# A hand-written planner for one Trainium2 core: new figures for durations, latencies and transfers, four projection tiles taken out of pairs, and another engine choice for late weight splits

## The chip, the cores and the metric

The kernel runs on one core of one Trainium2 chip. Time is device microseconds (us) of that core; lower is better. The engines are TensorE (PE, with its weight loads shown as PEld), VectorE (DVE), ScalarE (ACT), GpSimd (POOL) and SyncE (SP), which issues nearly all DMAs.

## The reference

One pre-norm layer over 512 tokens of 1024 channels with two token mixers in parallel, fed by one input projection. Cut to what matters:

```python
h = rmsnorm(x, norm_g)
(q_lat, c_kv, k_rope, z_a, q_b, k_b, v_b, z_b,
 q_idx, k_idx, w_idx, gate_a, gate_b) = split(h @ w_in)
# A: latent attention, 8 heads of 64 (+32 rotary), dense, chunk-causal
y_a = mla_attention(...) * silu(z_a)
# B: indexer scores, top 128 keys a query, T5 bias, 8 heads of 64
y_b = dsa_attention(...) * silu(z_b)
merged = sigmoid(gate_a) * (y_a @ w_o_a) + sigmoid(gate_b) * (y_b @ w_o_b)
out = rmsnorm(x + merged @ w_out, final_g)
```

All is float32. `z_b`, the gate path of the second mixer, is 512 channels wide: four tiles of 128 channels, called ZB here.

## The kernel before, in words

**Arithmetic.** A float32 operand is held as two parts: `hi`, the value rounded to PE's one-pass float32 format by an ACT cast (L370), and `lo = x - hi` by a subtraction on DVE (L401) or GpSimd (L403). A product is three matmuls, hi*hi, hi*lo and lo*hi (`mm3`). All weights come from HBM in float32 into four buffers `raw`, are split into slots `s_w` or `s_wo`, multiplied, and the slots freed. Slots are 73 tiles of 128 x 512 that every class of data shares (`SB`); PSUM has 8 banks, with limits by use.

**Stages.** Early projections (latents, indexer) from x; the normalised input `hT`; then a list of jobs (`QUEUE`): gate tiles `ga`/`gb`, gate paths `za`/`zb`, first-mixer weights `ma`, `va`, `pe`, second-mixer q and k `sb`, values `VB`; in between, the heads of both mixers; then `w_o` (16 jobs), and `w_out` as seven products (Strassen-Winograd, `out_job`, products 1 to 7), residual, final norm, output.

**Plain tiles and pairs.** A name in small letters in `QUEUE` is a plain tile (`proj`): 8 steps of k, three matmuls of 512 columns each. Two names in capitals form a pair (`proj2`): two tiles by 512 tokens are done as a 2 x 2 block product with seven half-size products, of 4 k steps and three matmuls of 256 columns each (`seven`). A pair needs sums of weight blocks (DVE or GpSimd), seven splits, sums of input blocks (`input_sums`, made once for all pairs, tiles `s_hs`), evictions of partial results (ACT) and two additions from PSUM (DVE). `silu2` finishes a ZB tile: tanh on ACT, one multiply on DVE; from PSUM for a plain tile, from SBUF for a pair.

**What sets the order.** No scheduler of the compiler does. The program's generator threads run through a planner (`Flow.run`) when the kernel is built: each step has an engine or a choice of engines and an assumed duration; the planner keeps when each engine comes free, adds a latency from engine to engine (`lat`) and a model of the DMA queue, and emits the step that it thinks can start first, weighted by a thread's priority. The order of emission is the order on each engine's in-order queue. For a step with a choice (`BOTH`: DVE or GpSimd) it takes the engine that ends first; `pbias` is added to GpSimd's end (0 by `soon`; `flow.pbias` where none is given, which becomes `LATE` after the last top-k). Two-input DVE steps and GpSimd steps exclude each other in the model (`shares`, `port`). In the model's figures `dur` of a DMA is its bytes at 360 GB/s.

**Names used further on.** `lg` banks hold attention logits (L1894 to L1896, exp by ACT L379); L498 are transposes; L413 is a scalar-tensor-tensor step on DVE; `s_wsum` sums of weight blocks; `bias_scratch<-s_sig` spills a gate tile to HBM, because `AWAY` holds all eight; `SUMS_AT` names the head after which `input_sums` starts, `PSUMS` its priority; `YSB` a head that releases the first mixer's output splits; `PHCAP`, `PCAP`, `SPARE` limit slots; `OUT_AT` says after which `w_o` jobs a `w_out` job is put; `PTOPK`, `PSCORE` are priorities (smaller is first).

Of the kernel before, what the change touches and what calls it, by code (L numbers as in the profile page):

```python
# [15 lines left out]
AF = mybir.ActivationFunctionType  # L16
# [137 lines left out]
class Flow:  # L154
    @staticmethod
    def lat(src, dst):

        if src == dst or src == "SP" or src is None:
            return 0.0
        if dst == "PE":  # L160
            return 0.26
        return {"PE": 0.2, "ACT": 0.15, "DVE": 0.16, "POOL": 0.08}[src]

    def __init__(self, order):
        self.free = {"PE": 0.6, "ACT": 0.73, "DVE": 0.93, "POOL": 0.73, "SP": 0.73}
# [48 lines left out]
    def run(self, stop=None):  # L214
        while self.threads:
# [36 lines left out]
            if eng == "SP":  # L252

                self.free["SP"] = s + 0.05
                self.hw = max(self.hw, s) + (0.65 if step.ins and step.outs else 0.475)
                self.dma = max(self.dma, self.hw + 0.65) + dur * (SLOWER[bool(step.ins and step.outs)] if s > 25.0 else 1.0)
                end = self.dma + (LAND if step.ins and step.outs else 1.5 if s < 0.77 or dur < 0.05 else 2.15 if s < 10.0 else 1.8 if s < 20.0 else 1.0) + step.late
            else:
                self.free[eng] = end = s + dur
                if self.shares(step, eng):  # L260
                    self.port, self.holder = end, eng
                    if eng == "DVE":
                        self.paired, self.pair = end, step.made
# [21 lines left out]
YIELD = 0.15  # L285
SWITCH = 0.1
JITTER = 0
SEED = 687
DRAWN = random.Random(SEED)
TC_ARGS = {}  # L290

# [2 lines left out]
def tile_block(ctx: ExitStack, tc: tile.TileContext, a: dict, out: bass.AP, bias_dram: bass.AP):  # L294
# [67 lines left out]
    def bufs(*vs):  # L362
        return [v.buf for v in vs if isinstance(v, View)]

    def act_opt(dst, src, func=AF.Copy, scale=None, bias=None, accum=None):
        t = (0.05 if in_ps(src) else 0.1) + 0.00083 * src.n + ((0.18 if in_ps(src) else 0.09) if accum is not None else 0) + (0.09 if isinstance(scale, View) else 0)

        def emit():
            if func == AF.Copy and scale is None:
                nc.scalar.copy(dst.ap, src.ap)  # L370
            else:
                kw = {}
                if scale is not None:
                    kw["scale"] = sc(scale)
                if bias is not None:
                    kw["bias"] = sc(bias)
                if accum is not None:
                    kw["accum_out"] = sc(accum)
                nc.scalar.activation(dst.ap, src.ap, func, **kw)  # L379

        return ("ACT", t, emit)
# [11 lines left out]
    def soon(step):  # L393
        step.pbias = 0.0
        return step

    def tt(dst, x, y, op, engs=("DVE",)):
        opts = []
        for e in engs:
            if e == "DVE":  # L400
                opts.append(("DVE", 0.07 + 0.00104 * x.n, lambda: nc.vector.tensor_tensor(dst.ap, x.ap, y.ap, op=op)))  # L401
            else:
                opts.append(("POOL", 0.15 + 0.0021 * x.n, lambda: nc.gpsimd.tensor_tensor(dst.ap, x.ap, y.ap, op=op)))  # L403
# [12 lines left out]
        return step  # L416

    def ts(dst, x, s1, s2, op0, op1=None):
        t = 0.1 + (0.00104 if in_ps(x) else 0.00052) * x.n
        kw = {} if op1 is None else {"op1": op1}  # L420
        step = Step([("DVE", t, lambda: nc.vector.tensor_scalar(dst.ap, x.ap, sc(s1), s2, op0, **kw))],
                    bufs(dst), bufs(x, s1))
        step.pair = not in_ps(x) and x.n > 8
        return step

    def scale_by(dst, x, s, engs=BOTH):

        opts = []
        for e in engs:
            if e == "DVE":  # L430
                t = 0.1 + (0.00104 if in_ps(x) else 0.00052) * x.n
                opts.append((e, t, lambda: nc.vector.tensor_scalar(dst.ap, x.ap, s.ap, None, ALU.mult)))
            elif e == "POOL":
                opts.append((e, 0.25 + 0.00083 * x.n,
                             lambda: nc.gpsimd.tensor_scalar(dst.ap, x.ap, s.ap, 1.0, ALU.mult, ALU.mult)))
            else:
                opts.append(act_opt(dst, x, AF.Copy, s))
        step = Step(opts, bufs(dst), bufs(x, s))
        step.pair = not in_ps(x)
        return step  # L440
# [27 lines left out]
        return step  # L468

    def stream(n):  # L470
        return max(0.0148 + n / 2400, 0.109) - 0.0015 * (n == 256)

    def mm(ps, pairs, start, stop, more=False):

# [17 lines left out]
    def turn(parts):  # L492


        def emit():
            for d, s in parts:
                product_to(d, True)
                nc.tensor.transpose(d.ap, s.ap, ident.tile)  # L498

        return pe(0.109 * len(parts), [d for d, _ in parts], [s for _, s in parts] + [ident.all], emit, len(parts))  # L500

    def dma(dst, src):

# [460 lines left out]
    def topk(i):  # L964

        n = P * (i + 1)
        work = mask_in_order(i)
        for r in range(TOPK // 8):
            m8 = yield Get(SMALL)
            t = 0.07 + 0.00104 * n  # L970
            yield Step([("DVE", t, lambda: nc.vector.max(m8.tile, work.ap))], [m8], [mask[i]])  # L971
            yield Step([("DVE", t + 0.068, lambda: nc.vector.match_replace(work.ap, m8.tile, work.ap, MARK))], [mask[i]], [m8])  # L972
            put(m8)
        yield ts(work, work, MARK, MASK, ALU.not_equal, ALU.mult)
        done.add(("mask", i))
# [1149 lines left out]
    def split_b(raw, key, last):  # L2125
        hi = yield slot("wo", 32)
        lo = yield slot("wo", 32)
        yield act(hi.all, raw)
        yield soon(lo_part(lo.all, raw, hi.all))
        if last:  # L2130
            put(raw.buf)
        right[key] = (hi, lo)
# [1 line left out]
    def out_job(product, c):  # L2134
# [3 lines left out]
        def prep(job):  # L2138
# [11 lines left out]
            else:  # L2150
                for i in range(2):
                    yield Until(lambda: 2 * c + i in sums)
                    t = sums[2 * c + i].all.f
                    yield soon(tt(t, raw[i], t, ALU.add if product == 6 else ALU.subtract, BOTH))
                    if i == 1:
                        put(job.raw)
                    yield from split_b(t, (product, 2 * c + i), product == 4)
# [405 lines left out]
```

## Time and profile before

| | us |
|---|---|
| median of 3 runs | 425.13 |
| lowest, highest | 423.97, 425.34 |
| the profiled execution | 425.56 |
| its span, first to last instruction | 423.8 |
| PE, DVE, ACT, POOL busy in it | 413.6, 378.7, 297.5, 100.9 |

The granted TensorE clock is 0.996 over the span. The page of the profile gives busy time by engine, the chain of work that ended last, groups of instructions and DMA issues; the trace behind it answers by stretch of time, by engine and by tile. A group's row reads: line, engine, operation, output<-inputs with buffer numbers left out, shapes, count, then busy us, mean ns of one, idle us of the engine before them and what ended that idle time. A row of the timeline reads: start us, length us, engine, line, operation, count, and in brackets the idle time before. A row of waits: who waited, for whom, total us, times, longest. A row of a stretch: its length, busy us of PE, PEld, DVE, ACT and POOL with instruction counts, granted clock, DMA share, GB/s. A matmul's end is modelled, and a matmul overlaps its neighbours in PE's pipeline, so the distance from start to start is what one costs.

### The profile page before, as it was taken

How to read it: one execution, taken by the hardware profiler on the slowest of the kernel's cores; microseconds unless marked ns; L12 is line 12 of the kernel's file. 1: busy time of each engine (PE TensorE's matmuls, PEld its weight loads, DVE VectorE, ACT ScalarE, POOL GpSimd, SP SyncE). 2: the span in 40 equal slices, each digit the busy share in tenths (PEclk: the TensorE clock that was granted, in tenths of full speed). 3: DMA queues.
4: the chain of work that ended last, by engine and by line, in shares of the span. 5: the costliest groups of instructions: out<-in, count | busy, mean ns of one | idle time of the engine just before them, and what ended most of it. 6: DMA issues, size and time to landing. Idle time of an engine off the chain costs nothing.

```text
span 423.8 us, 7541 instructions
## 1 busy us (share of the span) xinstructions
PE 413.6 (98%) x2487; PEld 368.8 (87%) x2487; DVE 378.7 (89%) x804; ACT 297.5 (70%) x682; POOL 100.9 (24%) x127
## 2 busy tenths in 40 slices
PE   9999999999999999999999999999999999999983
PEld 6999888898887888889999999999998888888863
DVE  4879789899999999997999789899869997999994
ACT  5796976479584967749786798997689744347534
POOL 1033764024344547541000012130001000010212
PEclk9999999999999999999999999999999999999998
DMA  8973345724644631442334737314633975566305
GB/s 266 394 285 101 116 137 183 182 57 110 202 104 152 179 111 49 125 113 76 113 130 105 200 95 199 95 65 136 187 113 125 336 254 200 182 201 209 134 1 199
DMA packets 30279, 65.91 MB, mean 156 GB/s; under 512 B 4648, under 2 KB 5688, under 8 KB 30240
## 3 DMA queue, kind: packets, MB, share of 16 engines
q1 hardware_dynamic: 29120, 63.82, 48.1%
q0 software_dynamic: 832, 1.22, 1.1%
q8 instruction: 19, 0.31, 0.3%
q10 hardware_dynamic: 288, 0.39, 0.3%
q14 instruction: 20, 0.16, 0.1%
HBM read 50.49 MB, written 4.21 MB: 129 GB/s over the span
## 4 chain that ended last, share of the span: by engine, by line
PE 65%; DVE 20%; ACT 5%; issue 4%; DMA 2%; POOL 1%; SPq 1%; POOLq 0%; DVEq 0%; ACTq 0%
PE ps L479 57%; PE ps L498 4%; DVE s_wo L401 2%; DVE s_mg L401 2%; ACT s_w L370 2%; DVE s_w L401 1%; DVE s_wsum L401 1%; DMA raw<-w_out 1%; DVE s_rg L401 1%; DVE s_x L413 1%; DVE mask L972 1%; DVE s_pair L401 1%; PE ps L606 1%; PE ps L946 1%; DVE s_xr L413 1%
## 5 line engine op out<-in xcount | busy, mean ns | idle before, releaser
L479 PE MATMUL ps<-s_h,s_w 128*128 128x512 f32 (+1 forms) x672 | 139.2, 350 | 0.0
L479 PEld LDWEIGHTS ps<-s_h,s_w 128*128 128x128 f32 x672 | 106.6, 189 | 13.4 <-ACT s_w L370 0.2
L370 ACT CAST s_w<-raw 128x512 fp32r<-128x512 f32 (+3 forms) x134 | 77.4, 596 | 18.5 <-DVE raw L401 9.3
L401 DVE TENSOR_TENSOR s_w<-raw,s_w 128x512 fp32r<-128x512 f32 (+2 forms) x104 | 67.1, 663 | 6.9 <-ACT s_w L370 6.2
L479 PE MATMUL ps<-s_hs,s_w 128*128 128x256 f32 x384 | 53.5, 285 | 0.0
L403 POOL TENSOR_TENSOR s_w<-raw,s_w 128x512 fp32r<-128x512 f32 (+2 forms) x30 | 35.0, 1173 | 77.6 <-DVE s_ys L413 36.9
L479 PEld LDWEIGHTS ps<-s_hs,s_w 128*128 128x128 f32 x384 | 49.2, 191 | 0.4
L479 PE MATMUL ps<-s_ys,s_w 128*128 128x512 f32 x192 | 43.7, 389 | 0.0
L479 PEld LDWEIGHTS ps<-s_ys,s_w 128*128 128x128 f32 x192 | 36.0, 188 | 7.6
L479 PE MATMUL ps<-s_wo,s_mg 128*128 128x512 f32 (+1 forms) x156 | 33.6, 374 | 1.2 <-ACT s_wo L370 0.9
L479 PEld LDWEIGHTS ps<-s_wo,s_mg 128*128 128x128 f32 x156 | 27.6, 188 | 7.0 <-ACT s_wo L370 1.3
L479 PE MATMUL ps<-s_w,s_xg 128*128 128x328 f32 (+1 forms) x192 | 32.9, 324 | 0.1
L479 PEld LDWEIGHTS ps<-s_w,s_xg 128*128 128x128 f32 x192 | 31.3, 188 | 0.6 <-ACT s_rbc L370 0.5
L379 ACT ACTIVATE s_p<-s_p,sm 128x512 f32<-128x512 f32 (+3 forms) x58 | 31.6, 564 | 0.1
L972 DVE MATCH_REPLACE8 mask<-sm,mask 128x256 f32<-128x256 f32 (+2 forms) x48 | 25.8, 540 | 0.0
L971 DVE MAX8 sm<-mask 128x8 f32<-128x256 f32 (+2 forms) x48 | 25.5, 547 | 0.3
L498 PE MATMUL ps<-ident,s_p 128*128 128x128 f32 x160 | 23.0, 274 | 0.0
L379 ACT ACTIVATE s_p<-ps,sm 128x128 f32<-128x128 f32 (+3 forms) x32 | 16.7, 525 | 8.9 <-DVE sm L1878 8.8
L370 ACT COPY s_tmp<-ps 64x512 f32<-64x512 f32 (+1 forms) x18 | 10.1, 562 | 15.5 <-PE ps L479 8.7
L498 PEld LDWEIGHTS ps<-ident,s_p 128*128 128x128 f32 x160 | 18.4, 140 | 2.6 <-DVE s_ph L401 0.5
L479 PE MATMUL ps<-s_lat,s_w 128*128 128x512 f32 x78 | 20.5, 394 | 0.0
L1977 DVE CUSTOM_DVE_ANT_0 s_p<-ps,mask 128x128 f32<-128x128 f32 (+3 forms) x32 | 15.3, 486 | 4.9 <-PE ps L479 4.7
(217 smaller groups left out, 798.4 us busy)
## 6 DMA issues: line engine op xcount, KB each, us to landing
raw<-w_out SPq DMA_DIRECT2D x18, 512.0 KB, 5.2
s_op<-s_op SPq DMA_DIRECT2D x36, 128.0 KB, 2.4
raw<-w_ga SPq DMA_DIRECT2D x8, 512.0 KB, 3.4
raw<-w_gb SPq DMA_DIRECT2D x8, 512.0 KB
raw<-w_o SPq DMA_DIRECT2D x16, 256.0 KB, 4.5
s_x<-xT SPq DMA_DIRECT2D x8, 256.0 KB, 4.0
s_xn<-x SPq DMA_DIRECT2D x8, 256.0 KB, 5.6
raw<-w_za SPq DMA_DIRECT2D x4, 512.0 KB, 5.0
```

Of the source, the lines that this page charges most:

```text
L370: nc.scalar.copy(dst.ap, src.ap)
L379: nc.scalar.activation(dst.ap, src.ap, func, **kw)
L401: opts.append(("DVE", 0.07 + 0.00104 * x.n, lambda: nc.vector.tensor_tensor(dst.ap, x.ap, y.ap, op=op)))
L403: opts.append(("POOL", 0.15 + 0.0021 * x.n, lambda: nc.gpsimd.tensor_tensor(dst.ap, x.ap, y.ap, op=op)))
L413: lambda: nc.vector.scalar_tensor_tensor(dst.ap, x.ap, sc(s), y.ap, op0=op0, op1=op1))],
L479: nc.tensor.matmul(ps.ap, l.ap, r.ap, start=start and i == 0, stop=stop and i == len(pairs) - 1, skip_group_check=more)
L498: nc.tensor.transpose(d.ap, s.ap, ident.tile)
L606: nc.tensor.matmul(ps.tile.rearrange("p (a b) -> p a b", b=P), z, z.rearrange("p (a b) -> p a b", a=1).to_broadcast([P, NT, P]), start=Tru ...
L946: yield pe(0.005 + n / 2400, [ps.all], [qs[h].all, ks[0].all], lambda: (product_to(ps[:, :n], True), nc.tensor.matmul(ps.tile[:, :n], qs[h ...
L971: yield Step([("DVE", t, lambda: nc.vector.max(m8.tile, work.ap))], [m8], [mask[i]])
L972: yield Step([("DVE", t + 0.068, lambda: nc.vector.match_replace(work.ap, m8.tile, work.ap, MARK))], [mask[i]], [m8])
L1977: step = Step([("DVE", 0.1 + 0.00104 * n, lambda: nc.vector.tensor_tensor_reduce(p.ap, ps.tile[:, :n], mask[i].tile, op0=ALU.add, op1=ALU. ...
```

## The change

It has three parts. The planner's figures: engine latencies, durations of some kinds of step, the DMA model after 25 us. The four ZB tiles: `ZB0` to `ZB3` (two pairs) become `zb0` to `zb3` (plain), at other places of the list. The engine choice of `w_out`'s sums and low parts: `soon` becomes `late`, which gives products 1, 7, 2, 6 and 5 a bias of 0 as before, and 4 and 3 the bias `LATE`; `LATE` itself goes from 0.75 to 0.4. Beside these, settings of priorities, slot limits and positions move.

```diff
 lat:
-            return 0.26
-        return {"PE": 0.2, "ACT": 0.15, "DVE": 0.16, "POOL": 0.08}[src]
+            return TO_PE
+        return {"PE": 0.2, "ACT": 0.14, "DVE": 0.12 if dst == "ACT" else 0.16, "POOL": 0.08}[src]
 run, a step of SP:
-                self.hw = max(self.hw, s) + (0.65 if step.ins and step.outs else 0.475)
-                self.dma = max(self.dma, self.hw + 0.65) + dur * (SLOWER[bool(step.ins and step.outs)] if s > 25.0 else 1.0)
-                end = self.dma + (LAND if step.ins and step.outs else 1.5 if s < 0.77 or dur < 0.05 else 2.15 if s < 10.0 else 1.8 if s < 20.0 else 1.0) + step.late
+                kind = 0 if step.ins and step.outs else 1 if step.outs else 2
+                if s > 25.0:
+                    at = max(self.hw, s)
+                    self.hw = at + 0.59
+                    self.dma = max(self.dma, at + 1.0) + dur * SLOWER[kind]
+                    end = self.dma + LAND[kind] + step.late
...
+    def few(x):
+        return 0.12 if x.ap.shape[0] < P else 0
 act_opt:
+        t += (0.1 if isinstance(bias, View) and not in_ps(src) else 0) + few(src) + (0.075 if func == AF.Square else 0)
+    def late(step, product):
+        step.pbias = 0.0 if product in EARLY else LATE
+        return step
 tt, on DVE:
-                opts.append(("DVE", 0.07 + 0.00104 * x.n, ...
+                opts.append(("DVE", 0.07 + 0.00104 * x.n + few(x), ...
 ts, scale_by: + few(x), 0.03 more with a tile as scalar
 stream:
-        return max(0.0148 + n / 2400, 0.109) - 0.0015 * (n == 256)
+        return max(0.0134 + n / 2400, 0.109)
 turn (a transpose): 0.109 -> 0.0875;  match_replace: t + 0.068 -> t - 0.009
 split_b:
-        yield soon(lo_part(lo.all, raw, hi.all))
+        yield late(lo_part(lo.all, raw, hi.all), key[0])
 out_job, products 6 and 4:
-                    yield soon(tt(t, raw[i], t, ALU.add if product == 6 else ALU.subtract, BOTH))
+                    yield late(tt(t, raw[i], t, ALU.add if product == 6 else ALU.subtract, BOTH), product)
...
-SEED = 687
+SEED = 1
-PHCAP = 6
+PHCAP = 5
-PTOPK = 15.0
-PSCORE = 12.0
+PTOPK = 13.0
+PSCORE = 10.0
-OUT_AT = (2, 3, 5, 10, 10, 10, 14)
+OUT_AT = (2, 3, 5, 9, 10, 11, 13)
-QUEUE = '... za2 za3 sb0 ga6 ga7 VB SB1 GB0 GB1 SB2 ZB0 ZB1 GB2 GB3 SB3 GB4 GB5 ZB2 ZB3 gb6 ou ou gb7 ou'
+QUEUE = '... za2 za3 sb0 zb0 ga6 ga7 VB SB1 GB0 GB1 SB2 zb1 zb2 GB2 GB3 SB3 GB4 GB5 zb3 gb6 ou ou gb7 ou'
-LATE = 0.75
+LATE = 0.4
+EARLY = (1, 7, 2, 6, 5)
-YSB = 7
+YSB = 5
-LAND = 2.6
-SLOWER = 1.08, 2.0
+LAND = 1.5, 1.3, 1.4
+SLOWER = 1.8, 1.13, 1.09
+TO_PE = 0.19
-SPARE = {'w': 2, 'wo': 6, 'sig': 3}
+SPARE = {'w': 3, 'wo': 6, 'sig': 3}
-PSUMS = 5.0
-PCAP = 10
+PSUMS = 8.0
+PCAP = 11
-SUMS_AT = ('a', 5)
+SUMS_AT = ('a', 6)
```

More of the change, by code (lines that the diff above doesn't have):

```diff
@@ L254, in run @@
                 self.free["SP"] = s + 0.05
-                self.hw = max(self.hw, s) + (0.65 if step.ins and step.outs else 0.475)
-                self.dma = max(self.dma, self.hw + 0.65) + dur * (SLOWER[bool(step.ins and step.outs)] if s > 25.0 else 1.0)
-                end = self.dma + (LAND if step.ins and step.outs else 1.5 if s < 0.77 or dur < 0.05 else 2.15 if s < 10.0 else 1.8 if s < 20.0 else 1.0) + step.late
+                kind = 0 if step.ins and step.outs else 1 if step.outs else 2
[4 more added lines that the diff above has]
+                    end = self.dma + LAND[kind] + step.late
+                else:
+                    self.hw = max(self.hw, s) + (0.475 if kind else 0.65)
+                    self.dma = max(self.dma, self.hw + 0.65) + dur
+                    end = self.dma + (1.5 if s < 0.77 or dur < 0.05 else 2.15 if s < 10.0 else 1.8 if s < 20.0 else 1.0) + step.late
             else:
@@ L400, in tt @@
             if e == "DVE":
-                opts.append(("DVE", 0.07 + 0.00104 * x.n, lambda: nc.vector.tensor_tensor(dst.ap, x.ap, y.ap, op=op)))
+                opts.append(("DVE", 0.07 + 0.00104 * x.n + few(x), lambda: nc.vector.tensor_tensor(dst.ap, x.ap, y.ap, op=op)))
             else:
@@ L418, in ts @@
     def ts(dst, x, s1, s2, op0, op1=None):
-        t = 0.1 + (0.00104 if in_ps(x) else 0.00052) * x.n
+        t = 0.1 + (0.00104 if in_ps(x) else 0.00052) * x.n + few(x) + 0.03 * isinstance(s1, View)
         kw = {} if op1 is None else {"op1": op1}
@@ L430, in scale_by @@
             if e == "DVE":
-                t = 0.1 + (0.00104 if in_ps(x) else 0.00052) * x.n
+                t = 0.13 + (0.00104 if in_ps(x) else 0.00052) * x.n
                 opts.append((e, t, lambda: nc.vector.tensor_scalar(dst.ap, x.ap, s.ap, None, ALU.mult)))
@@ L498, in emit @@
                 nc.tensor.transpose(d.ap, s.ap, ident.tile)
-        return pe(0.109 * len(parts), [d for d, _ in parts], [s for _, s in parts] + [ident.all], emit, len(parts))
+        return pe(0.0875 * len(parts), [d for d, _ in parts], [s for _, s in parts] + [ident.all], emit, len(parts))
     def dma(dst, src):
@@ L971, in topk @@
             yield Step([("DVE", t, lambda: nc.vector.max(m8.tile, work.ap))], [m8], [mask[i]])
-            yield Step([("DVE", t + 0.068, lambda: nc.vector.match_replace(work.ap, m8.tile, work.ap, MARK))], [mask[i]], [m8])
+            yield Step([("DVE", t - 0.009, lambda: nc.vector.match_replace(work.ap, m8.tile, work.ap, MARK))], [mask[i]], [m8])
             put(m8)
@@ L2436 @@
 QPOOL = 1
-PHCAP = 6
+PHCAP = 5
 WCAP = 12
 TCAP = 6
-PTOPK = 15.0
-PSCORE = 12.0
+PTOPK = 13.0
+PSCORE = 10.0
 PFILL = 12.0
 PHEAD = 4.0
-OUT_AT = (2, 3, 5, 10, 10, 10, 14)
+OUT_AT = (2, 3, 5, 9, 10, 11, 13)
 ORDER = [0,1,2,3]
-QUEUE = 'ga0 ga1 pe ma0 ga2 za0 va1 va0 ma1 ga3 za1 ma2 ga4 ga5 ma3 za2 za3 sb0 ga6 ga7 VB SB1 GB0 GB1 SB2 ZB0 ZB1 GB2 GB3 SB3 GB4 GB5 ZB2 ZB3 gb6 ou ou gb7 ou'
-LATE = 0.75
+QUEUE = 'ga0 ga1 pe ma0 ga2 za0 va1 va0 ma1 ga3 za1 ma2 ga4 ga5 ma3 za2 za3 sb0 zb0 ga6 ga7 VB SB1 GB0 GB1 SB2 zb1 zb2 GB2 GB3 SB3 GB4 GB5 zb3 gb6 ou ou gb7 ou'
+LATE = 0.4
+EARLY = (1, 7, 2, 6, 5)
 ADDED = 1.5
```

## The prediction

> **What bounds the kernel now.** I read the page first, then the stretches, then what TensorE (PE) waited for.
>
> ```profile
> span 423.8 us, 7541 instructions
> PE 413.6 (98%) x2487; PEld 368.8 (87%) x2487; DVE 378.7 (89%) x804; ACT 297.5 (70%) x682; POOL 100.9 (24%) x127
> ...
> PE 65%; DVE 20%; ACT 5%; issue 4%; DMA 2%; POOL 1%; SPq 1%; POOLq 0%; DVEq 0%; ACTq 0%
> ```
>
> PE is busy in 98% of the span; VectorE (DVE) is second, and the chain that ended last runs over it for 20%. A busy PE is partly modelled, so the stretches follow (columns: PE, weight loads, DVE, ACT, POOL).
>
> ```profile
> 190.00:250.00 60.00, 59.96 (x487) 58.82 (x487) 51.69 (x106) 48.34 (x115) 2.59 (x2) 1.00 0.40 122
> 250.00:330.00 80.00, 80.00 (x599) 75.87 (x598) 72.15 (x162) 68.99 (x169) 10.31 (x8) 1.00 0.44 131
> ...
> 347.00:398.00 51.00, 51.00 (x227) 42.15 (x226) 47.25 (x85) 25.71 (x48) 3.52 (x4) 1.00 0.62 206
> 398.00:417.00 19.00, 17.84 (x99) 14.95 (x97) 17.71 (x35) 8.63 (x21) 3.72 (x4) 1.00 0.04 15
> 417.00:424.00 7.00, 0.04 (x1) 0.00 (x0) 2.05 (x7) 2.82 (x6) 1.10 (x2) 0.77 0.69 261
> ```
>
> Between 190 and 398 us PE has practically no idle time, while DVE has 8 us free in each of the two middle stretches. So a us of matmuls put in there is a us of span, and a us taken from DVE there buys nothing directly. What can be won is where PE waits; the weight loads' side shows it best.
>
> ```profile
> PEld ps L479 <- ACT s_wo L370: 1.3, 1, 1.3
> PEld ps L1894 <- ACT s_p L379: 1.1, 1, 1.1
> ...
> PEld ps L498 <- DVE s_lat L413: 1.0, 1, 1.0
> PEld ps L479 <- DVE s_wo L401: 0.6, 1, 0.6
> PEld ps L479 <- ACT ps L370: 0.6, 3, 0.2
> ...
> PEld ps L479 <- DVE s_w L401: 0.2, 1, 0.2
> ```
>
> Four waits are of 0.6 us or more: 4.0 us. The rest (ten, from the fifth row down to the last, the warm-up aside) are 2.9 us. What a matmul takes, start to start, stands in the timeline of PE where nothing interrupts it:
>
> ```profile
> 298.68 1.60 PE L479 MATMUL ps<-s_h,s_w 128*128 128x256 f32 x12
> 300.12 1.60 PE L479 MATMUL ps<-s_hs,s_w 128*128 128x256 f32 x12
> ...
> 329.66 3.65 PE L479 MATMUL ps<-s_h,s_w 128*128 128x512 f32 x15
> 333.15 14.21 PE L479 MATMUL ps<-s_ys,s_w 128*128 128x512 f32 x62
> ```
>
> (300.12 - 298.68)/12 = 0.120 us at 256 columns; (333.15 - 329.66)/15 = 0.233 at 512 in a plain tile, where one is shown 3.65 - 14 x 0.233 = 0.39 us long; (14.21 - 0.39)/61 = 0.227 in the smoothest run. What each big wait costs in matmuls comes from three places of the timeline:
>
> ```profile
> 51.86 0.68 DVE L401 TENSOR_TENSOR s_tmp<-s_tmp,ropes 32x512 f32<-32x512 f32 x1
> ...
> 52.57 0.75 DVE L413 SCALAR_TENSOR_TENSOR s_lat<-ps,glat,s_lat 128x512 fp32r<-128x512 f32 x1
> ...
> 53.38 1.09 PE L498 MATMUL ps<-ident,s_latraw 128*128 128x128 f32 x8 [0.52 <-DVE s_lat L413]
> ```
> ```profile
> 135.21 0.58 ACT L370 COPY s_tmp<-ps 64x512 f32<-64x512 f32 x1 [5.87 <-DMA bias_scratch<-s_sig]
> ...
> 137.85 0.45 PE L1894 MATMUL ps<-s_op,qhi 100*128 100x384 f32 x1 [0.62 <-ACT s_p L379]
> 138.13 0.34 PE L1895 MATMUL ps<-s_op,qhi 96*128 96x384 f32 x1
> 138.31 0.34 PE L1896 MATMUL ps<-s_op,s_op 96*128 96x384 f32 x1
> ```
> ```profile
> 406.22 1.29 POOL L403 TENSOR_TENSOR s_wsum<-raw,s_wsum 128x512 f32<-128x512 f32 x1 [4.84 <-DVE s_xr L401]
> 406.84 0.63 ACT L379 ACTIVATE junk<-s_xr 128x512 f32<-128x512 f32 x1 [6.58 <-DVE s_xr L413]
> ...
> 408.55 0.60 ACT L370 CAST s_wo<-s_wsum 128x512 fp32r<-128x512 f32 x1
> ...
> 409.20 0.51 PE L479 MATMUL ps<-s_wo,s_mg 128*128 128x512 f32 x1 [0.88 <-ACT s_wo L370]
> ...
> 409.99 1.43 PE L479 MATMUL ps<-s_wo,s_mg 128*128 128x512 f32 x5 [0.28 <-DVE s_wo L401]
> ```
>
> The idle figure counts from the modelled end of the matmul before. A 512-wide one is shown 0.39 us long and starts every 0.23, so the lost time is idle plus 0.16: 0.68 at 53.4, 0.78 at 137.9, 1.04 at 409.2; at 409.99 it is 0.79 - 0.23 = 0.56. After a wait the second matmul comes late too (138.13 - 137.85 = 0.28 against 0.18 for the next), 0.1 a place. So: 0.8, 0.9 and 1.7 us. The loads' idle of 4.0 us stood for 3.1 us lost, 0.23 us less a wait; the ten small ones then lose 2.9 - 2.3 = 0.6 us.
>
> **The change, part by part.**
>
> *Four ZB tiles plain.* Before, ZB0/ZB1 and ZB2/ZB3 are two pairs: 7 products x 4 x 3 = 84 matmuls of 256 columns a pair. Plain, two tiles are 2 x 8 x 3 = 48 matmuls of 512 columns. A pair costs 84 x 0.120 = 10.1 us; two plain tiles 48 x 0.233 = 11.2, or 10.9 at 0.227. Two pairs: +1.6 to +2.2 us on PE, and no idle PE to hide it; I take +1.9. [...]
>
> ```profile
> L370 ACT CAST s_w<-raw 128x512 fp32r<-128x512 f32 x110 | 66.6, 621 | 17.6 <-DVE raw L401 9.3 <-DMA raw<-w_o 5.5 <-PE ps L479 2.0
> L401 DVE TENSOR_TENSOR s_w<-raw,s_w 128x512 fp32r<-128x512 f32 x89 | 59.7, 685 | 6.0 <-ACT s_w L370 5.3
> ...
> L370 ACT COPY s_pair<-ps 128x256 f32<-128x256 f32 x32 | 11.8, 369 | 7.8 <-PE ps L479 7.5
> ...
> L401 DVE TENSOR_TENSOR s_pair<-ps,s_pair 128x256 f32<-128x256 f32 x16 | 6.7, 419 | 1.1 <-PE ps L479 0.8 <-ACT s_pair L370 0.3
> ```
>
> Gone from each pair: four weight sums and three low parts (7 x 0.685), two 256-wide additions (2 x 0.419), three casts (3 x 0.621) and five evictions (5 x 0.369). For two pairs that is 11.3 us of DVE (some of it GpSimd's) and 7.4 us of ACT. They lie between 190 and 346 us, where PE did not wait for them but for fractions of a us: nothing directly, at best part of the 0.6 us of small waits; if DVE had been the bound there, it would be worth up to 11 us. The weight loads from HBM stay four of 512 KB. `zb0` goes ahead of `ga6`, so on SP's queue its load passes those of ga6, ga7 and VB's four; these come one load later, at a DMA share of 0.40 in that stretch. Each plain tile keeps its PSUM bank until tanh (ACT) and the multiply (DVE) have read it, and zb0's result holds its slot longer.
>
> *New figures in the planner.* They add no instruction; they decide each engine's order, and an order is kept by in-order queues, so a wrong figure shows as a wait. DVE steps on fewer than 128 partitions cost 0.07 + 0.53 = 0.60 us in the old figures, 0.72 in the new, 0.68 in the row at 51.86; three such steps stood ahead of the one that PE waited for at 53.4. The spill that ACT waited 5.87 us for:
>
> ```profile
> bias_scratch<-s_sig SPq DMA_DIRECT2D x8, 256.0 KB, 3.8
> ...
> s_op<-s_op SPq DMA_DIRECT2D x36, 128.0 KB, 2.4
> ```
>
> The old figures give a spill 0.475 + 0.65 + 0.79 + 1.0 = 2.9 us, the new 1.0 + 0.79 + 1.4 = 3.2, the trace 3.8; a 128 KB move 4.6 old, 3.2 new, 2.4 in the trace. All three move toward the trace, so I count the waits at 53.4 and 137.9 as gone: -0.8 and -0.9. What is late next: the same transposes and logits behind another PSUM bank; I put 0.5 us of new waits against it (nearest row: the small waits' 0.6), between 0 and the 3.1 that this kernel's big waits cost.
>
> *Late low parts.* Products 4 and 3 of w_out now count 0.4 us against GpSimd, and a square costs ACT 0.075 more. At 406.22 GpSimd makes the sum for product 4 in 1.29 us where DVE needs 0.69, and by 407.5 ACT is inside its squares and casts only at 408.55. With the sum on DVE the cast can stand ahead of the squares: -1.7 for both waits at 409 (between 0, where ACT's order stays, and 1.7). For all other late low parts `LATE` falls from 0.75 to 0.4, so more of those go to GpSimd (rival below).
>
> *Other settings* (slot limits, priorities, `SUMS_AT`, `YSB`, `OUT_AT`) move steps and their DMAs in time alone; at nothing, under the full PE of 190 to 398, except `SUMS_AT` (rival). The last 7 us, after the last matmul, keep their steps. `SEED` does nothing while `JITTER` is 0.
>
> **Sum.** Profiled execution 425.56 us, its span 423.8 and 1.8 around it: +1.9 - 1.7 - 0.9 - 0.8 - 0.6 (small waits) + 0.5 = -1.6, giving 424.0. The three runs have their median at 425.13, 0.43 lower: 423.5.
>
> **Rivals.**
> 1. *Only the wait at 409 goes*, the other two are replaced by their like: 425.1 + 1.9 - 1.7 - 0.4 = 424.9, no change. For it: an order of 2487 matmuls with only four big waits is hard to beat.
> 2. *Slower: the input sums come late.* They now start after head 6 of the first mixer, not 5, and at priority 8, not 5.
>
> ```profile
> L370 ACT CAST s_hs<-s_x x6: 602/621/635, 157.8 to 176.0; 128x512 fp32r<-128x512 f32 x6
> L401 DVE TENSOR_TENSOR s_hs<-s_tmp,s_hs x2: 679/910/1141, 184.4 to 186.0; 128x512 fp32r<-128x512 f32 x2
> ...
> L479 PE MATMUL ps<-s_w,s_hs x96: 278/283/467, 193.0 to 215.5; 128*128 128x256 f32 x96
> ```
> ```profile
> L403 POOL TENSOR_TENSOR s_y<-s_y,s_z x4: 1278/1298/1305, 110.1 to 183.7; 128x512 f32<-128x512 f32 x4
> ```
> They end by 187 and are first used at 193.0: 6 us of room, plus 5.6 of zb0's matmuls now ahead. A head takes (183.7 - 110.1)/6 = 12.3 us, so one head later all of it is spent and PE waits 0.7; a chain of 29 us that is a tenth longer makes it 3.6, and 427.1. It decides from 2.9 us on. Against it: the planner sees this wait.
> 3. *GpSimd holds DVE back.* A 512-wide subtraction on GpSimd is 1.29 us (row at 406.22) against 0.69, 0.6 more on whatever the two share. In the two stretches 347 to 417 DVE has 5.0 us free; from eight more such parts there (4.9 us) it decides, and at twelve (7.3) PE waits 2.3: 425.8. [...]
> 4. *The order around the three waits stays as it was*, the new figures being too near the old: 425.1 + 1.9 = 427.0.
>
> **Chances.** Forecast 0.49 (own range 422.1 to 424.5), rival 1 0.27, rival 2 0.12, rival 3 0.05, rival 4 0.07. A measurement of this kernel tells 0.3% (1.3 us) from no change: below 423.9 faster, above 426.4 slower. Faster 0.47 (0.02 of the forecast falls inside the bound), same 0.29, slower 0.24 with rival 3 counted at its worse end. Low end: all waits gone, plain tiles at +1.6: 425.1 + 1.6 - 4.0 = 422.7, less half of the runs' spread (425.34 - 423.97) and a further 0.5 for a shorter tail: 421.5. High end: rivals 2 and 4, 427.2.
>
> **What would show it.** Right: 2487 - 72 matmuls, four `s_z<-ps` more and no `s_z<-s_pair`; no PE wait above 0.5 us at the logits, the latents' transposes and s_wo; the product-4 sum on DVE; PE's last matmul near 415.5. Wrong: a PE wait for s_hs near 200 us, GpSimd busy above a tenth after 340 us, or as many big waits at other places.

## The result, and the profile after

The changed kernel is slower. In 20 runs of each kernel, taken in turn, it has a median of 428.2 us (425.5 to 431.3) against 424.9 (423.9 to 425.8) before: a ratio of 1.0082, 95% interval 1.0064 to 1.010, or 3.5 us. The forecast was 423.5 with a range of 421.5 to 427.2. The spread has grown with the median, from 1.9 to 5.7 us. The profiled execution took 427.18 us, span 425.3. Three single runs further down took 582 to 1446 us (two of before, one of tail_pool) and are left out of ranges and ratios.

The head of the page of after and its chain that ended last:

```profile
span 425.3 us, 7363 instructions
...
PE 415.6 (98%) x2415; PEld 366.8 (86%) x2415; DVE 371.7 (87%) x792; ACT 292.0 (69%) x663; POOL 97.8 (23%) x124
...
PE 65%; DVE 15%; DMA 10%; issue 4%; ACT 3%; SPq 2%; POOL 0%; POOLq 0%; DVEq 0%; ACTq 0%
```

PE has 72 matmuls fewer, as forecast, but is busy 2.0 us longer. DVE lost 7.0 us and ACT 5.5, and the time did not follow. DMA's share of the chain rose from 2% to 10%, spread over many transfers (`s_op<-kpel`, met below, has 1%). What the weight loads of PE waited for (in all, times, longest):

```profile
PEld ps L494 <- ACT ps L381: 1.5, 5, 0.5
...
PEld ps L494 <- DVE s_wo L416: 1.0, 1, 1.0
PEld ps L1909 <- ACT s_p L390: 0.8, 2, 0.5
PEld ps L494 <- ACT s_wo L381: 0.8, 1, 0.8
PEld ps L1910 <- DMA s_op<-kpel: 0.6, 1, 0.6
...
PEld ps L513 <- POOL rstd L468: 0.4, 1, 0.4
```

(Line numbers have moved: L370 is now L381, L401 is L416, L479 is L494, L1895 is L1910.) Two of the three big waits of before are gone: no row for `s_lat`, and only small ones for the logits' `s_p`. The third is not: both waits for `s_wo` stand here, 0.8 and 1.0. Among the new rows are two behind engines that no row of before names: the last part of the logits' operand (`s_op<-kpel`), which PE gets from a DMA, and `rstd`, which it gets from GpSimd. The small waits for ACT at PSUM banks (`ACT ps`) sum to 1.5 us here, 0.6 before, and 0.7 in a second execution of after.

A sum over all matmuls tells more than the rows. I take each one's start less the start before it, and call what goes beyond the undisturbed spacing of its shape (0.109 us at 128 columns, 0.120 at 256, 0.228 at 512 and so on) lost, if it is over 0.04 us. From the first matmul after the warm-up to the last (the split into lost and rest moves by up to 0.4 us with the spacings one takes, alike in every row; the differences between rows stay):

| execution | stream, us | lost, us | rest, us |
|---|---|---|---|
| before, as in the prediction | 411.85 | 11.84 | 400.0 |
| before, a second one | 411.79 | 11.77 | 400.0 |
| after | 413.52 | 11.48 | 402.0 |
| after, a second one | 413.13 | 11.19 | 401.9 |

So PE's own work grew by 2.0 us, and the waits hardly shrank in sum: they moved. That leaves two questions. Where do the other 1.5 us of the median come from, which these executions do not show? And why did a new order, made from figures nearer to the trace, not shorten the waits?

### The profile page after: what moved, and what is told of

The parts are those of the page before. It is cut to its first block, busy times and chain, and to the rows that moved or that the text cites. A ratio compares the mean times of both kernels' runs of the same rounds, so it can differ in the third digit from the quotient of the medians.

```text
span 425.3 us, 7363 instructions
## 1 busy us (share of the span) xinstructions
PE 415.6 (98%) x2415; PEld 366.8 (86%) x2415; DVE 371.7 (87%) x792; ACT 292.0 (69%) x663; POOL 97.8 (23%) x124
## 4 chain that ended last, share of the span: by engine, by line
PE 65%; DVE 15%; DMA 10%; issue 4%; ACT 3%; SPq 2%; POOL 0%; POOLq 0%; DVEq 0%; ACTq 0%
PE ps L494 56%; PE ps L513 5%; DVE s_w L416 3%; SPq L523 2%; DVE s_wo L416 2%; DVE s_wsum L416 2%; DMA raw<-w_ql 1%; DMA s_xn<-x 1%; DMA s_x<-xT 1%; DMA s_fg<-final_g 1%; ACT s_w L381 1%; DMA s_op<-kpel 1%; DMA raw<-w_o 1%; PE ps L1910 1%; PE ps L1909 1%
## 5 line engine op out<-in xcount | busy, mean ns | idle before, releaser
L494 PE MATMUL ps<-s_h,s_w 128*128 128x512 f32 (+1 forms) x696 | 156.1, 364 | 0.0
L494 PEld LDWEIGHTS ps<-s_h,s_w 128*128 128x128 f32 x696 | 113.5, 189 | 15.3 <-DVE s_w L416 0.4
L381 ACT CAST s_w<-raw 128x512 fp32r<-128x512 f32 (+3 forms) x130 | 74.7, 594 | 21.2 <-DMA raw<-w_o 12.9
L416 DVE TENSOR_TENSOR s_w<-raw,s_w 128x512 fp32r<-128x512 f32 (+2 forms) x97 | 62.6, 667 | 10.2 <-ACT s_w L381 8.7
L418 POOL TENSOR_TENSOR s_w<-raw,s_w 128x512 fp32r<-128x512 f32 (+2 forms) x33 | 39.3, 1193 | 73.2 <-PE ps L513 30.0
L494 PE MATMUL ps<-s_ys,s_w 128*128 128x512 f32 x192 | 44.0, 390 | 0.2 <-DVE s_pair L428 0.2
L494 PEld LDWEIGHTS ps<-s_ys,s_w 128*128 128x128 f32 x192 | 35.8, 188 | 8.0 <-issue 0.6
L494 PE MATMUL ps<-s_hs,s_w 128*128 128x256 f32 x288 | 39.2, 284 | 0.0
L494 PEld LDWEIGHTS ps<-s_hs,s_w 128*128 128x128 f32 x288 | 36.5, 191 | 0.1
L494 PE MATMUL ps<-s_wo,s_mg 128*128 128x512 f32 (+1 forms) x156 | 33.6, 374 | 1.0 <-DVE s_wo L416 0.7
L494 PEld LDWEIGHTS ps<-s_wo,s_mg 128*128 128x128 f32 x156 | 27.6, 188 | 6.9 <-DVE s_wo L416 1.0
L494 PE MATMUL ps<-s_w,s_xg 128*128 128x328 f32 (+1 forms) x192 | 32.8, 324 | 0.1
L494 PEld LDWEIGHTS ps<-s_w,s_xg 128*128 128x128 f32 x192 | 31.4, 188 | 0.5 <-ACT s_rbc L381 0.5
L390 ACT ACTIVATE s_p<-s_p,sm 128x512 f32<-128x512 f32 (+3 forms) x54 | 29.9, 575 | 0.0
L494 PE MATMUL ps<-s_lat,s_w 128*128 128x512 f32 x78 | 20.7, 397 | 0.0
```

The lines of the kernel that those rows point to most:

```text
L416: opts.append(("DVE", 0.07 + 0.00104 * x.n + few(x), lambda: nc.vector.tensor_tensor(dst.ap, x.ap, y.ap, op=op)))
L494: nc.tensor.matmul(ps.ap, l.ap, r.ap, start=start and i == 0, stop=stop and i == len(pairs) - 1, skip_group_check=more)
```

## Experiments

Each kernel ran beside the kernel before on one chip, 5 rounds unless said. Theory P says that the plain tiles' price on PE is the loss and that the waits only change place; theory W, that the new order has waits on transfers that differ from execution to execution. Theories M, D and E came later, with the second half of the runs.

**The changed kernel again.** No edit.

> The changed kernel, not altered, for a second profile and times beside the others. Theory P (the plain ZB tiles cost 1.9 us on PE, the waits are merely replaced, and nothing else matters): every execution has the same waits, so span and time agree with the first profile, 425.3 and 427.2 us, within 0.5 us. Rival W (some of the new order's waits depend on when DMAs land, and differ from execution to execution): the time lies anywhere between 425.5 and 431, and the PE waits of this profile are at other places or of other sizes than in the first, most of all behind DMAs.

428.26 us (426.66 to 431.38), ratio 1.0096 (1.0066 to 1.0127). Its waits in the profiled execution, the same order as above:

```profile
PEld ps L1910 <- DMA s_op<-kpel: 1.2, 1, 1.2
PEld ps L513 <- POOL rstd L468: 1.1, 1, 1.1
```

The same instructions in the same order lose twice as much at the DMA here, and 0.7 us more at `rstd`. W holds for these two places.

**Queue and figures apart.** Two kernels: after with the old queue (pairs), before with the new one (plain tiles).

```
after_pairs:   QUEUE = '... GB1 SB2 ZB0 ZB1 GB2 ...'         (in after.py)
before_plain:  QUEUE = '... sb0 zb0 ga6 ... SB2 zb1 zb2 ...'  (in before.py)
```

> The changed kernel with the list of tiles of the kernel before: ZB0 to ZB3 as two pairs again, everything else as changed. Theory P: PE loses 1.9 us of matmuls, so 428.2 - 1.9 = 426.3 us. Rival W: the waits stay, and the DVE and ACT work of the pairs (11 and 7 us) comes back under settings that were not made for it: not faster than 428, with several new waits of PE for s_w and pair results between 190 and 350 us; up to 438 if they come as densely as the planner's own timeline for this kernel has them (18 us of PE waits).

> The kernel before with the changed list of tiles alone: four plain ZB tiles, old figures and settings. Theory P: 424.9 + 1.9 = 426.8 us, with as few waits as before. Rival W (a list and settings go together): further waits between 190 and 340 us, 428 to 431 us; the planner's own timeline has 5.7 us of PE waits here against 1.8 for the kernel before.

440.74 us (ratio 1.0387, 1.0361 to 1.0412) and 432.8 (1.0186, 1.0143 to 1.023), both slower than either expectation. By the sum over matmuls, after_pairs loses 26.5 us and before_plain 18.0, for 11.8 in before, while the rest is 400.2 and 402.1: the plain tiles' 2 us again, under either set of figures. Not all of the loss is waits: the profile of after_pairs has one stretch of 3.4 us at half clock (granted 0.50 from 319.8 to 323.0, 0.94 in the mean of 300 to 330) and that of before_plain two (317.7 to 321.0, 341.6 to 344.9; 0.990 in the mean of the span), up to 1.7 us each. Neither half of the change can be read from these times; a queue, the figures and the other settings fit one another, and one of them alone spoils the order. That is why the next kernels keep an order and change single instructions.

**GpSimd as before.**

```
-LATE = 0.4                    +LATE = 0.75
-EARLY = (1, 7, 2, 6, 5)       +EARLY = (1, 7, 2, 6, 5, 4, 3)
```

> The changed kernel with the engine choice of late parts as before: LATE 0.75, and no bias against GpSimd for products 4 and 3. If GpSimd's share of the late parts cost the time: 426.7 us or less. If it has no part in it, as GpSimd's busy time of 97.8 us against 100.9 suggests: within 1 us of 428.2, and the two waits for s_wo near 410 us remain, 1.4 us together or less.

428.29 us (426.09 to 429.11), ratio 1.0077 (1.0052 to 1.0103): no difference from after, so the choice of engine for late low parts costs and brings nothing. But its profiled execution (span 427.2) shows what can follow the wait at the DMA. The timeline of PE, and two stretches of this run (columns: PE, weight loads, DVE, ACT, POOL, granted clock, DMA share, GB/s):

```profile
84.81 0.33 PE L1910 MATMUL ps<-s_op,qhi 96*128 96x128 f32 x1 [1.40 <-DMA s_op<-kpel]
...
86.00:90.50 4.50, 4.50 (x25) 4.50 (x25) 3.18 (x10) 2.71 (x9) 0.00 (x0) 0.62 0.02 5
90.50:95.00 4.50, 4.50 (x32) 4.21 (x31) 4.38 (x12) 2.71 (x8) 1.32 (x2) 1.00 0.00 0
```

PE stood for 1.5 us, went on, and 2 us later was granted a clock of 0.62 in the mean over 4.5 us: half clock for (1 - 0.62) x 4.5 / 0.5 = 3.4 us (from 86.8 to 90.1 it reads 0.50), or 1.7 us lost with PE busy. Wait and clock together took 3.2 us in this execution, twice the wait's own length.

**A us of PE alone.** Before, with 16 extra matmuls of 256 columns in the two ZB pairs, four at a time, whose sums the next matmul overwrites: 16 x 0.120 = 1.9 us more PE, everything else in place.

```
+            for _ in range(again):
+                ...
+                nc.tensor.matmul(ps.ap, pairs[0][0].ap, pairs[0][1].ap, start=True, stop=False, ...)
```

> The kernel before, same order on every engine, with 16 matmuls of 256 columns more in the two ZB pairs: the first matmul of two products of each pair is issued five times instead of once (it starts its sum anew each time, so the result is the same). 16 x 0.120 = 1.9 us of PE, the price of the plain ZB tiles. Theory P (a us of PE is a us of time): +1.9 us against the kernel before, 426.5 to 426.9. If PE's queue had room between 260 and 330 us: under +0.6.

425.97 us (425.49 to 427.36), ratio 1.0039 (1.0027 to 1.005), or 1.7 us. The extra matmuls stand at 246, 251, 302 and 307 us. A us of PE there is nearly a us of time, and the plain tiles' 2.0 us of PE explain about half of the loss.

**Without the wait for `rstd`.** The planner keeps a GpSimd instruction that comes soon behind a DVE step on two SBUF tiles in order with it. For `rstd` this puts GpSimd behind a row of weight sums in after, and did not in before (timelines of POOL, after first):

```profile
27.35 1.29 POOL L468 TENSOR_TENSOR rstd<-rstd,neghalf 128x4 f32<-128x4 f32 x1 [24.68 <-DVE s_w L416]
```
```profile
24.39 1.04 POOL L453 TENSOR_TENSOR rstd<-rstd,neghalf 128x4 f32<-128x4 f32 x1 [21.71 <-DVE rstd L445]
```

```
-                    elif step.fenced and self.pair:
+                    elif step.fenced and self.pair and not step.free:    # free: rstd
```

> The changed kernel, same order on every engine; the one GpSimd step that makes rstd (the inverse square root, 128 x 4) no longer gets the planner's extra dependency on the last two-input DVE step ahead of it. Theory W: rstd is ready for it at about 23.4 us, and it runs at 24 instead of 27.4 to 28.0; PE's wait at the rstd transposes (0.3, 0.9 and 1.0 us in three profiles) and half of the one for s_rbc behind it go: 0.7 to 1.0 us off the median, 427.3. Rival P (waits are alike in both kernels): no change, since DVE's splits in the first 30 us then give back what is won.

428.08 us (426.96 to 429.75), ratio 1.0078 (1.0055 to 1.0101). The wait is gone from the trace and nothing came of it; in the profiled execution the wait at the DMA was 1.6 us. Whether the time won at `rstd` was paid there is not shown: the move was issued 0.6 us earlier than in after_again and PE came 0.7 us earlier, but the move took longer.

**Without the wait for the DMA.** On SP's queue of after, a weight load and the spill stood ahead of the move that the first logits need. The timelines of SP and PE of after, where `kpel` is issued at 78.91 and the matmul that reads it starts at 83.57:

```profile
77.01 0.86 SPq L523 DMA_DIRECT2D s_op<-kpeh  x1
77.98 0.41 SPq L523 DMA_DIRECT2D raw<-w_ga  x1
78.44 0.42 SPq L523 DMA_DIRECT2D bias_scratch<-s_sig  x1
78.91 0.57 SPq L523 DMA_DIRECT2D s_op<-kpel  x1
```
```profile
82.88 0.22 PE L1909 MATMUL ps<-s_op,qhi 100*128 100x128 f32 x1
83.57 0.33 PE L1910 MATMUL ps<-s_op,qhi 96*128 96x128 f32 x1 [0.47 <-DMA s_op<-kpel]
```

In before, load and spill stood ahead as well, but the move was issued 5.4 us ahead of its matmul; in after it is 4.0 us ahead of the time at which the matmul was due (82.88 + 0.06). SP and PE of before:

```profile
80.23 0.57 SPq L508 DMA_DIRECT2D s_op<-kpel  x1
```
```profile
85.64 0.28 PE L1895 MATMUL ps<-s_op,qhi 96*128 96x128 f32 x1
```

That is the new figure for moves at work. Worked by hand through the planner's queue (an estimate from its figures), the new ones let the first `kpel` move land 1.0 + 1.65 (load) + 0.79 (spill) + 0.33 (move) + 1.5 - 1.18 (issued that much behind the load) = 4.1 us after its issue, and 4.0 us is the lead that it got. The same sum with the old figures and before's order gives 5.3, and the lead was 5.4. On the chip the matmul could start only 4.7 (after), 5.5 (after_again and after_pool) and 5.8 us (after_nofence) after the issue. The figure came nearer to the median landing of the 128 KB moves (2.4 us in before; 4.6 old, 3.2 new), and left no room for this one. The edit issues the two (load and spill) behind the first two `kpel` moves, all other orders kept:

```
+            if eng == "SP" and self.nth_sp in (70, 71):    # load, spill: issued after SP's step 74
+                self.held_back.append(emit)
```

> The changed kernel, same order on PE, DVE, ACT and GpSimd; on SP's queue the load raw<-w_ga and the spill bias_scratch<-s_sig that stand ahead of the first two s_op<-kpel moves are issued behind them. Theory W: the moves land 0.9 us earlier and PE's wait for them near 84 us (0.6, 1.2 and 1.5 us in three profiles, one of them with 3.4 us of half clock behind it) shrinks to 0 to 0.6: 0.8 to 1.3 us off the median, 427.1, and less spread. Rival P: no change.

426.59 us (426.15 to 427.29), ratio 1.0046 (1.0031 to 1.0061). 1.6 us off the median, more than expected, and the wait is gone. Its six runs spread over 1.1 us (after_again's six over 4.7). Its SP and PE:

```profile
78.29 0.57 SPq L536 DMA_DIRECT2D s_op<-kpel  x1
```
```profile
83.24 0.22 PE L1922 MATMUL ps<-s_op,qhi 100*128 100x128 f32 x1
83.30 0.28 PE L1923 MATMUL ps<-s_op,qhi 96*128 96x128 f32 x1
```

The move is issued 0.6 us earlier, and ahead of a load of 512 KB and a spill of 256 KB; that was worth nearly half of the loss. Both edits together:

> The changed kernel with both of these edits. Theory W: they add up: 1.5 to 2.2 us off, 426.3, which is the kernel before plus the 1.7 us of PE work of the plain tiles. Rival P: no change. If W is half right (the first wait delays the second, so that one takes the place of the other): 427.2.

426.2 us (425.03 to 429.63), ratio 1.0044 (1.0025 to 1.0064): what is left over before, 1.6 to 1.9 us, is what before_extra gave for the plain tiles. But its twelve runs spread over 4.6 us, with the wait at `kpel` gone as well, so that wait alone does not make the spread. The slowest runs of after_again, after_nofence and after_both (431.4, 429.8 and 429.6 us) and one of the three slowest of after (430.4) have a mean granted clock of 0.991, while the runs of before beside the first three have 0.994 or more. A stretch of 3.4 us at half clock takes 0.004 off the mean (3.4 x 0.5 / 428), so by this estimate one lies in these runs too, in after_both without the wait at `kpel`. None of them was profiled, and that stays open.

**How long the waits of before are.** The prediction sized them in one execution. A second one, a single run:

> The kernel before, unchanged: a second profiled execution of it. Theory M (the waits that the prediction wanted to remove were long in the one execution that it read, and shorter in most): the waits at 53.4, 137.9 and 409 us sum to 0.9 to 1.8 us (in the kernel with 16 more matmuls, which has the same order, they were 0.24, 0.23 and 0.81), and the span is 422 to 423.5. Rival: the prediction's sizes are typical, the three places sum to 2.8 us or more as in the first execution (3.1 to 3.4), and the span is 423.5 to 424.5.

Its waits of the weight loads:

```profile
PEld ps L1894 <- ACT s_p L379: 1.1, 1, 1.1
...
PEld ps L479 <- ACT s_wo L370: 0.9, 1, 0.9
PEld ps L479 <- DVE s_wo L401: 0.6, 1, 0.6
...
PEld ps L498 <- DVE s_lat L413: 0.5, 1, 0.5
```

425.42 us, span 423.7. From start to start: 0.25 us lost at the transposes near 53 (0.69 in the prediction's execution), 0.85 at the logits near 138 (0.79), 0.67 and 0.56 at 409 (1.04 and 0.56). With before_extra, which keeps the order, and before_tail below: 0.24 to 0.26 near 53, 0.23 to 0.85 near 138. Theory M expected 0.9 to 1.8 us at the three places and its rival 2.8 or more; 2.3 is between them.

**Without the waits at 409.** In before, three squares on ACT go behind the two casts of w_out, and three multiplications by final_g on DVE behind four low parts.

```
+HELD = {"DVE": ((693, 694, 695), 699), "ACT": ((580, 581, 582), 584)}    # these steps are issued after that one
```

> The kernel before; at its end alone, three squares on ScalarE are issued behind the two casts of w_out, and three multiplications by final_g on VectorE behind four low parts, which PE waits for at 409. Theory M: only 0.8 us of waits typically lie there, half of them go: 0.3 to 0.5 us, ratio to before 0.9988 to 0.9995. Rival, the prediction's term: 1.7 us lie there, 0.9 to 1.5 us go, ratio 0.9965 to 0.998.

424.79 us (423.82 to 425.91), ratio 1.0007 (0.9998 to 1.0017): no gain, which neither theory had expected. The edit did what it should: where PE waited twice in before (first fence, the second execution), before_tail goes through, and its last group ends 1.7 us earlier.

```profile
409.06 0.50 PE L479 MATMUL ps<-s_wo,s_mg 128*128 128x512 f32 x1 [0.51 <-ACT s_wo L370]
409.85 1.45 PE L479 MATMUL ps<-s_wo,s_mg 128*128 128x512 f32 x5 [0.29 <-DVE s_wo L401]
411.13 5.79 PE L479 MATMUL ps<-s_wo,qhi 128*128 128x512 f32 x36
```
```profile
407.73 1.80 PE L492 MATMUL ps<-s_wo,s_mg 128*128 128x512 f32 x7
409.38 5.80 PE L492 MATMUL ps<-s_wo,qhi 128*128 128x512 f32 x36
```

Yet the time stayed. The chain of before (in order of time: start, us, what) says why, and I had not read it there:

```profile
406.14 1.26 DVE s_xr L413 x3
407.41 1.33 DVE s_rg L401 x3
408.73 2.41 DVE s_wo L401 x4
411.14 1.20 DVE s_xr L413 x2
412.34 1.20 DVE s_rg L401 x2
```

From 388 us, where `s_wsum`, `s_wo` and `s_part` begin to follow one another, up to 414, the chain runs on DVE, but for one cast on ACT (0.6 us) and some 4 us that the profile puts down as issue. PE's waits at 409 lie beside it. In before_tail DVE does the same steps in another order and is through 0.46 us earlier than in the second execution of before, not 1.7. Theory D: DVE's queue sets the end. Its rival E: a fixed tail behind PE's last matmul, and something else took the 1.7 us. Two more kernels settle it, each before_tail with the same time added to one engine or the other.

```
tail_dve:  DVE steps 702, 703 (s_rg<-s_xr,s_fg, 512 wide) issued twice
tail_pe:   PE steps 1094, 1098, 1102 (three matmuls each) issued twice
```

> The kernel of before_tail (in which PE waits at 409 no longer and ends its matmuls 1.7 us earlier), with two of VectorE's 512-wide multiplications by final_g near 412 issued twice: 1.2 us more on VectorE, same results. Theory D (from about 388 us on VectorE's queue sets the end, PE's waits at 409 lie beside it): 1.0 to 1.4 us above before_tail, 425.7 to 426.2, ratio to before 1.0025 to 1.004. Rival E (the end is set by PE's last matmul and a fixed tail behind it, and something else took the 1.7 us): VectorE has room there, 424.5 to 425.0.

> The kernel of before_tail with the first three matmuls of each of the last three groups of PE issued twice (three of 512 columns, six of 256): 1.4 us more on PE behind 409, same results. Theory D: VectorE reads these banks later than PE ends them even so (1.1 us of room for the first, 0.3 to 0.9 for the others): 424.5 to 425.1, ratio 1.000 to 1.001. Rival E: 1.2 to 1.5 us above before_tail, 425.9 to 426.4.

(Unlike what was expected, some of the doubled products in tail_pe enter their sum twice, so in those banks it computes something else; its instructions are of the same kind and size.) tail_dve: 426.56 us (425.91 to 426.6, five runs), ratio 1.0047 (1.0035 to 1.0059). By the ratios that is 1.7 us above before_tail, more than theory D's 1.0 to 1.4, for 1.5 us more on DVE (2.74 us in the first row below, 1.29 in before_tail). tail_pe: 424.52 us (424.06 to 426.44), ratio 1.0006 (0.9995 to 1.0016), nothing for 1.4 us of PE. Theory D holds, E falls. DVE of tail_dve, and PE of tail_pe with its nine further matmuls:

```profile
411.13 2.74 DVE L416 TENSOR_TENSOR s_rg<-s_xr,s_fg 128x512 f32<-128x512 f32 x4
...
414.23 0.68 DVE L428 SCALAR_TENSOR_TENSOR s_xr<-ps,s_xr 128x512 f32<-128x512 f32 x1
```
```profile
408.69 7.21 PE L494 MATMUL ps<-s_wo,qhi 128*128 128x512 f32 x45
```

In after the chain is not the same. In both its profiles it leaves DVE at the second wait for `s_wo` and runs over PE's last matmuls; the chain of the first:

```profile
411.01 0.61 DVE s_wo L416
411.62 0.04 issue
411.67 4.24 PE ps L494 x17
415.91 0.02 issue
415.93 0.70 DVE s_xr L428
```

DVE waits 0.27 us for PE ahead of the step at 415.93. So a part of PE's wait is on the chain there, but by this trace no more than these 0.3 us of it could be won before DVE's own queue sets the end again.

**Taking time from DVE there.** before_tail with one of the three held multiplications (512 wide) on GpSimd, ahead of the other two or behind them.

> The kernel of before_tail with one 512-wide multiplication by final_g moved from VectorE to GpSimd, behind VectorE's last low part of w_out, where VectorE reads PSUM for 1.2 us. Theory D: 0.6 us leave VectorE's queue, 0.3 to 0.6 us off before_tail, 424.1 to 424.5, ratio to before 0.9988 to 1.0. Rival E: no change, 424.8; if GpSimd keeps VectorE from its next steps, 0.3 to 0.7 us above before_tail.

> As tail_pool, with the multiplication on GpSimd behind the two 256-wide ones on VectorE, so that it runs while VectorE reads PSUM for 1.2 us and not beside a multiplication of two SBUF tiles. Theory D, with the reading of tail_pool that a GpSimd instruction and a VectorE instruction on two SBUF tiles wait for one another: 0.5 to 0.6 us leave VectorE's queue and none come back, 0.3 to 0.6 us off before_tail, ratio to before 0.9988 to 0.9998, a version below both kernels. Rival: GpSimd holds VectorE's PSUM reads too or its next multiplications, 0.2 to 1.2 us above before_tail, ratio 1.001 to 1.003.

Ahead: 425.93 us (425.21 to 426.22), ratio 1.0029 (1.0019 to 1.0039), about 1 us worse than before_tail. Behind: 424.33 (423.74 to 425.77), ratio 0.9995 (0.9983 to 1.0007), which no longer differs from before. GpSimd and DVE of the first, then of the second:

```profile
409.88 1.35 POOL L420 TENSOR_TENSOR s_rg<-s_xr,s_fg 128x512 f32<-128x512 f32 x1 [2.73 <-DVE s_wo L418]
```
```profile
409.65 1.86 DVE L418 TENSOR_TENSOR s_rg<-s_xr,s_fg 128x256 f32<-128x256 f32 x2
```
```profile
409.97 1.30 POOL L421 TENSOR_TENSOR s_rg<-s_xr,s_fg 128x512 f32<-128x512 f32 x1 [3.40 <-DVE s_rg L419]
```
```profile
409.07 0.75 DVE L419 TENSOR_TENSOR s_rg<-s_xr,s_fg 128x256 f32<-128x256 f32 x2
409.74 1.28 DVE L431 SCALAR_TENSOR_TENSOR s_xr<-ps,s_xr 128x512 f32<-128x512 f32 x2
```

Two 256-wide multiplications take 0.75 us alone and 1.86 with GpSimd running; DVE's two reads of PSUM take 1.28 beside GpSimd, and 1.27 in the first kernel, where GpSimd is through. So the two multiplications took 1.1 us longer in tail_pool, beside a GpSimd instruction of 1.35 us. In the second kernel too DVE's next two multiplications, which GpSimd's end overlaps, take 1.48 us instead of 1.28.

**Settings found anew.** Two kernels whose settings came from a search for the earliest planned end: before_found with the old figures and pairs, after_found with plain tiles and the new figures, but the old one for moves.

```
before_found:  QUEUE '... ga5 ma3 ...' (one exchange), YIELD 0.2, PREST 4.5, SPARE w 2 wo 7 sig 3, PSUMS 1.5
after_found:   LAND 2.6, SLOWER 2.0 (moves), OUT_AT, FENCE 4.0, YSA 3, YSB 4, PREST -1.0, SPARE w 4 wo 6 sig 4, za3/za2 exchanged
```

> The kernel before with its old figures and pairs, and five other settings (one exchange in the queue of w loads, YIELD, PREST, SPARE, PSUMS), for which its planner ends 0.6 us earlier (416.6 for 417.2) and plans 1.2 us of PE waits for 1.8. If the planner's end tells the chip's time to half a us: 424.0, ratio 0.9986. If waits on the chip come from what the planner does not know: 423.5 to 426.5, either way.

> The kernel after (plain ZB tiles) with the old figure for moves between SBUF tiles (LAND 2.6, SLOWER 2.0) and all its other new figures, and settings found for this mix, for which the planner ends at 413.4 (after: 414.5). Theory P (plain tiles cost 1.7 us, and the tight move figure the wait for the last part of s_op near 84 us): that wait is gone, the median lies 1.0 to 2.5 us below the kernel after, 425.7 to 427.2, and still above before, ratio 1.002 to 1.006. Rival (the new figures as such are the gain, and the move figure alone spoilt it): below before, 423.0 to 424.2.

before_found: 426.42 us (423.72 to 427.53), ratio 1.0033 (1.0015 to 1.0051), though PE's last matmul starts at 414.94 there, 1.7 us earlier than in the second execution of before: the planned end is no measure of the time, and once more an earlier end of PE is not an earlier end. What makes it slower than before in the median its one profile (span 423.8) doesn't show; that is open. after_found: 426.01 us (424.66 to 427.38), ratio 1.0033 (1.002 to 1.0045): with the old move figure the first `kpel` move is issued 5.0 us ahead of its matmul and there is no wait for it; the kernel lies 2.2 us below after and still above before, as theory P has it; the other new figures bring nothing that can be seen.

No version ended measurably below before. tail_pool_late comes nearest.

## Why the prediction was wrong, point by point

1. *Plain tiles, +1.9.* Right: PE's work without waits grew by 2.0 us, and 1.9 us of matmuls added alone raised the time by 1.7. "No idle PE to hide it" holds where the matmuls were added, from 246 to 307.
2. *The wait at 409, -1.7.* This is the step that failed. It went wrong twice. The order there did not change as argued: the sum for product 4 went to DVE, as foretold, but DVE put it behind `s_xr` and `s_rg`, and the casts stayed late. From start to start 0.52 and 0.94 us are lost at 410.5 and 411.7, against 1.04 and 0.56 before. And the term could not have paid: with both waits taken away in before_tail, the time rose by 0.2 us, with an interval around nothing. The argument "what can be won is where PE waits" is true only where PE is on the chain. The row that denied it stood in the prediction (DVE busy 17.71 of the 19 us from 398 to 417), and I used it only for rival 3. The number that the step needed was the same stretch in the chain.
3. *The waits at 53.4 and 137.9, -0.8 and -0.9.* Both are gone in after; whether the figures for few partitions and spills did it was not tested apart. Their size was read from a single execution. Other executions of the same order lose 0.25 and 0.23 to 0.85 there, so 0.5 to 1.1 us were to be had, not 1.7, and other waits took their place.
4. *New waits, +0.5.* Too small, and in the wrong place: I looked for them at banks and logits. "All three move toward the trace" was read from the 128 KB moves (2.4 us); for the 64 KB move that PE waits for, behind a load and a spill, the new figures come to 4.1 us, where it took 4.7 to 5.8. The wait at `kpel` near 84 us costs 0.6 to 1.6 us by itself, and in one execution the clock behind it took 1.7 more. Removing it is worth 1.6 us of the median. At `rstd` 0.3 to 1.0 us came on top, from an order between GpSimd and DVE; alone it moved nothing.
5. *Small waits, -0.6.* Not gained; all that PE loses sums to 11.8 before and 11.5 after.

The sum with what was measured: +2.0 (PE; 1.7 by before_extra), +1.6 (`kpel` with its clock, by after_kpel), nothing at 409, and 0 to 0.3 for all other waits that came and went, which is what after_kpel and after_both stand above before beyond the 1.7 of before_extra: 3.3 to 3.9, for 3.5 measured. The last term is a remainder, so the sum closes in part by its making; what stands by itself is before_extra.

Of the rivals, the one that ended slower (the input sums late, PE waiting near 200) did not occur: the first matmul on `s_hs` starts at 201.3 instead of 193.0, and no time is lost ahead of it in either kernel. GpSimd holding DVE did show, 1.1 us in tail_pool, but after_pool shows that the engine choice for late low parts is no part of this loss. The sums of rivals 2 and 4, 427.1 and 427.0, came nearest, for other reasons. None of the rivals had a DMA that lands later than planned.

## What to carry to other kernels

Before a wait on the busiest engine is put down as time to be won, follow the chain through that stretch: if another engine is on it, the wait lies beside it, and adding a us to each engine in turn shows this with two kernels. A planning figure for a transfer should not be fitted to a median alone: the move that PE waited for was given 4.0 us and took 4.7 to 5.8, behind a load and a spill. When such a figure is made smaller, the late landings meet the engine that waits. Sizes of single waits want two or three executions, since here the same order lost 0.23 us at one place in one and 0.85 in the next.

## What the hardware did that I had not expected

A wait of 1.5 us on PE was followed by 3.4 us at half clock (granted 0.62 over 4.5 us), together 3.2 us and not 1.5. It need not be: waits of 0.6, 1.2 and 1.6 us at the same place in three other executions (after twice, after_nofence) were followed by a clock of 1.00. In after_pairs, which has a stretch at half clock too, no wait of the weight loads was longer than 1.4 us; in before_plain, which has two, the longest were 2.7 and 1.5. The length of a wait alone does not decide it; what does, no run here separates. And GpSimd, with 1.35 us of its own work, stretched two multiplications of DVE from 0.75 to 1.86 us.
